# Layer 1's gate and up projections by Strassen's algorithm in a two-layer diffusion block: seven half products for eight

## The chip, the cores and the metric

The kernel runs on one core of one Trainium2 chip. The metric is the device time of one execution in microseconds (us). Profiles show the same kernel with the hardware profiler on, and give the span from the first to the last instruction.

## The reference, cut to what matters

Two layers work on 512 latent tokens and 256 context tokens of width 1024, in fp32. Each has a mixer (an mLSTM, a gating MLP, a convolution, then an output projection) and a SwiGLU feed-forward network (FFN). The second layer, layer 1, computes the mixer's output and the FFN for the latent tokens alone. What the change touches is this, with `FFN_HIDDEN` = 2816:

```python
def swiglu(h, w_gu, w_down):
    gate, up = jnp.split(h @ w_gu, 2, axis=-1)
    return (jax.nn.silu(gate) * up) @ w_down
...
x = x + g2 * swiglu(rmsnorm(x, norm2_g[l]) * (1.0 + sc2) + sh2, w_gu[l], w_down[l])
```

## The kernel before, in words

Everything lies transposed: features on the 128 partitions, tokens along the free dimension. A product of fp32 numbers is made of three passes of a faster format (`fp32r`): each operand is split into a rounded part `hi` and a remainder `lo`, and TensorE accumulates hi times hi, hi times lo and lo times hi in PSUM (L379, L380, L381, in `mm` inside `tiles`, L362). A weight tile of 128 columns by 1024 rows (8 slices of k, 128 rows each) arrives by DMA in a `raw` buffer (L314), ScalarE makes `hi` (L339) and VectorE makes `lo` (L320, `split_lo`). Three `raw` buffers and four `hi`/`lo` pairs (`spl`) rotate (`BUFFERS`, L217). The normalized activations lie in `HA` (latent) and `HB` (context), hi and lo each.

In layer 1 the 512 latent tokens form two groups of 256 (`GX0`, `GX1`), and every matmul there has 256 columns. The FFN has 22 hidden tiles of 128 (`NJ`); each takes one gate column tile and one up column tile (`gu_col`, L1569), so a pair of column tiles and both token groups cost 2 x 2 x 8 x 3 = 96 matmuls. `gu_evac` (L1579) then makes the hidden tile: silu on ScalarE (L1590), the product with up on VectorE (L1593), the split into hi (L1597, ScalarE) and lo (L1599, VectorE). The down projection is done in three runs over groups of hidden tiles (`FFN_GROUPS`, L35: 8, 7 and 7 tiles); `d_run` (L1603) makes 8 output tiles by 2 token groups a run, and VectorE adds each to the residual `xT` (L749). The last run starts with two output tiles side by side over k, so that the last hidden tile is read late.

The order of the work isn't written out by hand: `Plan` (L42) runs cooperating threads against a table of costs (`PE`, `DVE2`, `ACT` and so on) and writes each engine's instructions in the order in which its own clock serves them. TensorE follows the list of `steps`; VectorE and ScalarE take whatever thread is ready first. On the chip each engine then runs its list strictly in that order and waits on semaphores. The norm in front of the FFN is `norm` and `norm_lo` (L739, L714, L716); they write `HA`.

Of the kernel before, what the change touches and what calls it, by code (L numbers as in the profile page):

```python
# [14 lines left out]
P = 128  # L15
# [19 lines left out]
FFN_GROUPS = ((0, 8), (8, 7), (15, 7))  # L35
# [181 lines left out]
BUFFERS = {"ps": 8, "slot": 10, "raw": 3, "spl": 4, "pb": 4, "wi": 3, "cp": 1, "kk": 2, "hc": 2, "C0": 5, "C1": 5}  # L217
# [3 lines left out]
def backbone(ctx, tc, xT_d, cT_d, wmod_d, wb_d, wgv_d, wv_d, wout_d, wgu_d, wd_d, sw_d, sb_d, cv_d, rv_d, id_d, mk_d, out_d):  # L221
# [44 lines left out]
    # ---------------------------------------------------------------- weights  # L266
# [8 lines left out]
    def wsrc(key):  # L275
# [12 lines left out]
        if kind == "d":  # L288
            j0, n = FFN_GROUPS[key[2]]
            return wd_d[key[1], key[3], :, j0 * P:(j0 + n) * P], n, P  # L290
# [10 lines left out]
    def loader():  # L301
        for i, key in enumerate(ORDER):
            if key[0] == "x":
# [3 lines left out]
                continue  # L307
            src, a, b = wsrc(key)
# [14 lines left out]

    def splitter():
        for i, key in enumerate(ORDER):
            if key[0] == "x":
                continue
# [14 lines left out]
    prog = []  # L342

# [18 lines left out]
    def tiles(items, lead, lag, nk, src, wait=None, order=None, depth=3, wide=False, mid=None, after=None, ahead=2):  # L362
        """Steps of a run of 128-column products, tokens in one or two groups, `lead` ahead of `lag`.
        items: (weight key, evac, prio). With `wide`, the first tiles share one pass over k."""
# [42 lines left out]
        def multi(idx, pairs, state, spans):  # L407
            """pairs: (tile, group, first slot); one pass over the slots in spans, newly taken weights idx"""
# [187 lines left out]
    # ---------------------------------------------------------------- norms  # L596
# [161 lines left out]
    # ---------------------------------------------------------------- one layer  # L758
# [9 lines left out]
    def layer(l):  # L768
# [26 lines left out]
        # gates and the v half of the SGU, tokens on partitions  # L795
# [247 lines left out]
        # gated depthwise convolution  # L1043
# [92 lines left out]
        # mLSTM projections  # L1136
# [427 lines left out]
        steps.append(spawn_gs(l, 1))  # L1564
        steps += tiles([out_col(d) for d in range(KD)], gl, gg, KD, hsrc, lambda k, g: E("ys", g["t0"], k), YK, wide=True, ahead=AHEAD[1])

        hid, gups = {}, {}

# [9 lines left out]

        def gu_evac(j, g, pg, pu):  # L1579
# [23 lines left out]
        def d_run(gi):  # L1603
# [15 lines left out]
            def after(g):  # L1619
                st["dn", gi] = st.get(("dn", gi), 0) + 1  # L1620
                if st["dn", gi] == 2:
                    release("slot", nj)
# [172 lines left out]
```

## Time and profile before

| what | value |
|---|---|
| time, median of 3 runs | 1578.63 us (1578.39 to 1581.98) |
| span of the profiled execution | 1579.7 us (no separate time is listed for it) |
| instructions | 25862 |
| TensorE busy | 1549.2 us (98%), 10712 matmuls |
| VectorE busy | 845.3 us (54%) |
| ScalarE busy | 539.7 us (34%) |
| layer 1's FFN, about 1192 to 1570 us | 3168 matmuls of 256 columns |

Engines are PE (TensorE), PEld (its weight loads), DVE (VectorE), ACT (ScalarE), POOL and SP. Matmuls overlap in the pipe: one of 256 columns is shown with 0.28 us, while the next begins 0.11 to 0.12 us later, so the count of matmuls in a window says more than their busy time. The same holds to a lesser degree for VectorE and ScalarE, whose neighbouring instructions overlap by some 0.1 us. A wait is shown in brackets behind the instruction, with what ended it.

### The profile page before, as it was taken

What the parts mean: (1) busy time and instruction counts of PE and PEld (TensorE: products, weight loads), DVE (VectorE), ACT (ScalarE), POOL (GpSimd) and SP (SyncE); (2) the same over time, 40 slices, a digit from 0 to 9 for tenths busy, and PEclk for the clock granted to TensorE, in tenths of its full rate; (3) what the DMA queues carried; (4) which work ended last, traced back from release to release, by engine and by line L of the source; (5) the groups of instructions that cost most, each with busy time, mean ns of one, the idle gap of its engine ahead of it and who ended that gap; (6) DMA issues with size and microseconds to landing.
All of it is one profiled execution on the core that took longest, in us unless ns stands there. A gap on an engine that the chain in (4) does not pass through costs nothing.

```text
span 1579.7 us, 25862 instructions
## 1 busy us (share of the span) xinstructions
PE 1549.2 (98%) x10712; PEld 1386.1 (88%) x10712; DVE 845.3 (54%) x1739; ACT 539.7 (34%) x1055; POOL 32.0 (2%) x50
## 2 busy tenths in 40 slices
PE   5999999999999999999999999999999999999998
PEld 4887889889888888888888888788999999999997
DVE  5359877456655555344444363686766334334334
ACT  4332367534222212221122233426745321231333
POOL 0000010000000000000000000000100000000000
PEclk9999999999999999999999999999999999999999
DMA  9343345312333334333343122213332232223222
GB/s 327 118 131 118 121 131 159 120 59 68 107 120 128 113 107 144 134 108 101 132 151 121 52 83 81 87 55 113 103 107 81 94 94 94 94 88 99 96 83 66
DMA packets 68209, 173.22 MB, mean 110 GB/s; under 512 B 7052, under 2 KB 18428, under 8 KB 68092
## 3 DMA queue, kind: packets, MB, share of 16 engines
q1 hardware_dynamic: 65324, 170.15, 33.3%
q8 instruction: 84, 1.38, 0.4%
q10 hardware_dynamic: 2768, 1.42, 0.3%
q14 instruction: 33, 0.27, 0.1%
HBM read 169.34 MB, written 2.21 MB: 109 GB/s over the span
## 4 chain that ended last, share of the span: by engine, by line
PE 95%; DVE 2%; DMA 1%; issue 1%; ACT 0%; SPq 0%; POOLq 0%; POOL 0%; DVEq 0%
PE mm L379 27%; PE mm L380 27%; PE mm L381 27%; PE vp L1150 2%; PE vp L1152 1%; PE vp L1151 1%; PE stp L1287 1%; PE num L1371 1%; PE num L1374 1%; PE modps L501 1%; PE gvp L823 1%; PE gvp L824 1%; PE gvp L825 1%; DVE lo L320 1%; PE sT L1350 1%
## 5 line engine op out<-in xcount | busy, mean ns | idle before, releaser
L379 PE MATMUL mm<-HA,hi 128*128 128x256 f32 (+1 forms) x1568 | 525.3, 335 | 0.0
L380 PE MATMUL mm<-HA,hi 128*128 128x256 f32 (+1 forms) x1568 | 516.7, 330 | 2.4 <-DVE HA L716 1.8
L381 PE MATMUL mm<-HA,lo 128*128 128x256 f32 (+1 forms) x1568 | 516.2, 329 | 0.4 <-DVE lo L320 0.4
L320 DVE TENSOR_TENSOR lo<-raw,hi 128x1024 fp32r<-128x1024 f32 (+2 forms) x202 | 240.4, 1193 | 299.6 <-ACT hi L339 292.3
L339 ACT CAST hi<-raw 128x1024 fp32r<-128x1024 f32 (+2 forms) x202 | 206.3, 1024 | 565.7 <-PE mm L380 302.3
L381 PEld LDWEIGHTS mm<-HA,lo 128*128 128x128 f32 x1568 | 295.9, 189 | 30.6 <-DVE lo L320 0.6
L380 PEld LDWEIGHTS mm<-HA,hi 128*128 128x128 f32 x1568 | 296.2, 189 | 26.9 <-DVE HA L716 2.7
L379 PEld LDWEIGHTS mm<-HA,hi 128*128 128x128 f32 x1568 | 294.6, 188 | 28.7 <-issue 4.3
L379 PE MATMUL mm<-hid,hi 128*128 128x256 f32 (+1 forms) x704 | 218.7, 311 | 0.0
L381 PE MATMUL mm<-hid,lo 128*128 128x256 f32 (+1 forms) x704 | 217.5, 309 | 0.0
L380 PE MATMUL mm<-hid,hi 128*128 128x256 f32 (+1 forms) x704 | 217.2, 308 | 0.0
L379 PE MATMUL mm<-HB,hi 128*128 128x256 f32 x592 | 170.0, 287 | 0.0
L380 PE MATMUL mm<-HB,hi 128*128 128x256 f32 x592 | 164.6, 278 | 0.0
L381 PE MATMUL mm<-HB,lo 128*128 128x256 f32 x592 | 164.5, 278 | 0.0
L749 DVE SCALAR_TENSOR_TENSOR xT<-mm,modc,xT 128x256 f32<-128x256 f32 (+1 forms) x128 | 69.9, 550 | 160.1 <-PE mm L381 159.1
L379 PEld LDWEIGHTS mm<-hid,hi 128*128 128x128 f32 x704 | 132.7, 188 | 8.2 <-issue 0.8
L381 PEld LDWEIGHTS mm<-hid,lo 128*128 128x128 f32 x704 | 132.4, 188 | 7.7
L380 PEld LDWEIGHTS mm<-hid,hi 128*128 128x128 f32 x704 | 132.4, 188 | 7.5
L379 PEld LDWEIGHTS mm<-HB,hi 128*128 128x128 f32 x592 | 111.3, 188 | 8.1 <-issue 4.6
L380 PEld LDWEIGHTS mm<-HB,hi 128*128 128x128 f32 x592 | 111.9, 189 | 3.0 <-DVE HB L716 0.2
L381 PEld LDWEIGHTS mm<-HB,lo 128*128 128x128 f32 x592 | 111.2, 188 | 0.0
L573 DVE SCALAR_TENSOR_TENSOR macc<-raw,csil,macc 128x512 f32<-128x512 f32 x140 | 101.5, 746 | 0.6
(230 smaller groups left out, 1534.4 us busy)
## 6 DMA issues: line engine op xcount, KB each, us to landing
raw<-in_wmod SPq DMA_DIRECT2D x96, 512.0 KB, 3.8
raw<-in_wgu SPq DMA_DIRECT2D x88, 512.0 KB, 3.5
raw<-in_wb SPq DMA_DIRECT2D x36, 512.0 KB, 3.7
raw<-in_wd SPq DMA_DIRECT2D x32, 448.0 KB, 3.3
pbt<-dr SPq DMA_DIRECT2D x40, 256.0 KB, 3.4
raw<-in_wout SPq DMA_DIRECT2D x16, 512.0 KB, 3.6
raw<-in_wd SPq DMA_DIRECT2D x16, 512.0 KB, 3.6
raw<-in_wv SPq DMA_DIRECT2D x8, 512.0 KB, 3.9
```

Of the source, the lines that this page charges most:

```text
L320: dve.tensor_tensor(lo, r, hi.bitcast(F32), ALU.subtract)
L339: act.copy(hi, RAW[i])
L379: pe.matmul(o, lhsT=hi[:, k, :], rhs=hh, start=(j == 0), stop=False)
L380: pe.matmul(o, lhsT=hi[:, k, :], rhs=hl, start=False, stop=False)
L381: pe.matmul(o, lhsT=lo[:, k, :], rhs=hh, start=False, stop=(j == nk - 1))
L501: pe.matmul(p[32 * c:32 * c + 32, 0:256], lhsT=csil[:, k, :], rhs=s[:, c, :], start=(k == 0), stop=(k == KD - 1), skip_group_check=True)
L573: dve.scalar_tensor_tensor(a[:, g, :], s[:, i, :], c, a[:, g, :], ALU.mult, ALU.add)
L749: dve.scalar_tensor_tensor(x, p[:, 0:n], MODC[l][:, v, d, g:g + 1], x, ALU.mult, ALU.add)
L823: pe.matmul(out, lhsT=hh, rhs=hi[:, kk, :], start=(k == 0), stop=False)
L824: pe.matmul(out, lhsT=hh, rhs=lo[:, kk, :], start=False, stop=False)
L825: pe.matmul(out, lhsT=hl, rhs=hi[:, kk, :], start=False, stop=(k == KD - 1))
L1150: pe.matmul(out, lhsT=hh, rhs=hi[:, kk, :], start=(k == 0), stop=False)
```

## The change

Layer 1's first two hidden tiles (`NPLAIN`) are computed as before. For each of the other 20, the gate and the up tile form a matrix of two by two blocks (two column tiles by two halves of k), the activations another (two halves of k by two token groups), and the product is made in Strassen's way (Winograd's form of it): seven products of 4 slices of k by 3 passes, 12 matmuls each, so 84 for 96. The pieces are:

- `pair_sums` (new, L343): loads both raw tiles of a pair, makes four sums of weight quarters in place on VectorE (128x512 each), and splits three full tiles (U1, U2, U3) and one half tile (U4, kept in a part of `HA` that is free after the plain tiles).
- `t_forms` (new, L1725): once, makes the four sums of activation quarters (four 128x1024 additions of hi and lo, then four sums, then four splits on ScalarE and VectorE), after the norm has ended. They lie in `HB` and in memory that was slots before.
- `pair_steps`, `pair_end`, `product` (new): the order of the seven products in TensorE's list. Three PSUM banks a pair, A, B and C. Products 1, 6, 7 and 4 accumulate into A one after the other, and between them ScalarE copies A's state out (`copy_out`, L1840); product 5 and the closing product go to C, product 2 to B. VectorE joins the copies with B and C (`join_one`, L1858; L1855). The end of a pair stands behind the first product of the next.
- `pair_out` (new, L1866): a last sum, silu over 512, two products on VectorE, the split of the hidden tile over 512.
- The down projection runs over four groups of 6, 6, 5 and 5 hidden tiles; the first three are woven into four pairs each, so that twelve pairs carry pieces of it between their products and eight don't.
- Buffers: `raw` 3 to 4, `spl` 4 to 5, for the whole kernel, so the planner may load and split weights earlier in layer 0 too. An argument of the build, `dynamic_dma_scratch_size=1024`, makes the room.

TensorE's list goes from 10026 matmuls to 9786, VectorE's from 1741 instructions to 1936, ScalarE's from 1030 to 1103.

```diff
-FFN_GROUPS = ((0, 8), (8, 7), (15, 7))
+FFN_GROUPS = (((0, 8), (8, 7), (15, 7)), ((0, 6), (6, 6), (12, 5), (17, 5)))
+NPLAIN = 2
...
-BUFFERS = {"ps": 8, "slot": 10, "raw": 3, "spl": 4, "pb": 4, "wi": 3, "cp": 1, "kk": 2, "hc": 2, "C0": 5, "C1": 5}
+BUFFERS = {"ps": 8, "slot": 10, "raw": 4, "spl": 5, "hp": 0, "u4": 0, "pb": 4, "wi": 3, "cp": 1, "kk": 2, "hc": 2, "C0": 5, "C1": 5}
...
+    def pair_sums(key, us):
...
+        yield from cast(0, r1)
+        yield from cast(3, a22)
+        yield from low(0, r1)
+        yield from low(3, a22)
+        yield from add(a22, a21, a22)
+        yield from add(a21, a11, a21)
+        yield W(ev("u", key[:3], 1))
+        yield from cast(1, r2)
+        yield from add(a11, a22, a11)
+        yield from add(a12, a11, a12)
+        yield W(ev("u", key[:3], 2))
+        yield from cast(2, r1)
+        yield from low(1, r2)
+        release("raw")
+        yield from low(2, r1)
+        release("raw")
...
+        def t_forms():
+            for g in (gl, gg):
+                for k in range(KD):
+                    yield W(ev("h", l, 1, g["t0"], k))
+            yield W(E("ffnmem"))
+            f = st.pop("tf")
+            for x, q in enumerate(((0, 0), (0, 1), (1, 0), (1, 1))):
+                yield DVE2(1024)
+                dve.tensor_tensor(f[x], quarter(0, *q).bitcast(F32), quarter(1, *q).bitcast(F32), ALU.add)
...
+            def first(w):
+                yield A("ps")
+                q["A"], q["U1"] = ps("bA"), w
+                yield from product(q["A"], w, 0, (0, 0), True)
+                spawn(copy_out(j, 0), 0.6)
+
+            def fifth(w):
+                yield A("ps")
+                q["C"], q["U2"] = ps("bC"), w
+                yield from product(q["C"], w, 1, 0, True)
+
+            def sixth(w):
+                q["U3"] = w
+                yield W(E("cp", j, 0))
+                yield from product(q["A"], w, 0, 1, False)
+                spawn(copy_out(j, 1), 0.6)
...
+            def seventh():
+                yield W(E("cp", j, 1))
+                yield from product(q["A"], q["U2"], 0, 2, False)
+                release("spl")
+                spawn(copy_out(j, 2), 0.6)
+
+            out = [([key + (0,)], first)]
+            if before is not None:
+                out.append(pair_end(before))
+            return out + [([key + (1,)], fifth), ([key + (2,)], sixth), ([], second), ([], seventh)]
...
+                yield W(E("cp", j, 2))
+                yield from product(q["A"], w, None, 3, False)
+                U4.append(w)
+                release("u4")
+                yield W(E("join", j))
+                yield from product(q["C"], q["U3"], 1, (1, 1), False)
+                release("spl")
+                spawn(pair_out(j), 0.5)
...
+            blocks = [pair_steps(j, j - 1 if i else None) for i, j in enumerate(pairs)]
+            for gi, (j0, nj) in enumerate(fg[:-1]):
+                first, ds = j0 + nj - NPLAIN + 1, d_run(gi)
+                for b in range(4):
+                    part = ds[b * len(ds) // 4:(b + 1) * len(ds) // 4]
+                    blocks[first + b] = blocks[first + b][:2] + spread(blocks[first + b][2:], part)
```

What the planner makes of it is seen at three places of VectorE's list. The first is the start of layer 1's FFN, behind the last `lo` of the norm (L716 before, L790 now). Before, the evacuations of the first tiles (`s`, `hid`) and the splits of the next weights (`lo<-raw,hi`) follow:

```order
L716 SCALAR_TENSOR_TENSOR HA<-nt,modc_84,HA 128x256 x2
L1593 TENSOR_TENSOR s<-s,mm 128x256 x2
L1599 TENSOR_TENSOR hid<-s,hid 128x256 x2
L320 TENSOR_TENSOR lo<-raw,hi 128x1024 x2
L1593 TENSOR_TENSOR s<-s,mm 128x256
```

Now six wide additions (`tf`) and seven evacuations of the plain tiles (L1691, L1697) come first, and behind them these rows. `tf` are the activation sums, `HB<-tf,HB` the remainders of the first two of them, `raw<-raw` the weight sums of the first two pairs; the third row from the end is the remainder of U2 of the first pair, which TensorE's second Strassen product reads:

```order
L1749 SCALAR_TENSOR_TENSOR tf<-tf 128x1024
L1751 SCALAR_TENSOR_TENSOR tf<-tf 128x1024
L1691 TENSOR_TENSOR s<-s,mm 128x256
L354 TENSOR_TENSOR lo<-raw,hi 128x1024 x2
L354 TENSOR_TENSOR HA<-raw,HA 128x4x128 x2
L359 TENSOR_TENSOR raw<-raw 128x512 x4
L1741 TENSOR_TENSOR HB<-tf,HB 128x1024
L359 TENSOR_TENSOR raw<-raw 128x512 x4
L1741 TENSOR_TENSOR HB<-tf,HB 128x1024
L354 TENSOR_TENSOR lo<-raw,hi 128x1024
L1697 TENSOR_TENSOR ffn<-s,ffn 128x256
L354 TENSOR_TENSOR lo<-raw,hi 128x1024
```

So all activation sums and the weight work of two pairs stand in one line ahead of the second product's weights. The second place is one period of the pairs that carry no down projection. Before, VectorE had this between two tiles there:

```order
L1593 TENSOR_TENSOR s_11464<-s_11464,mm_11435 128x256
L1593 TENSOR_TENSOR s_11495<-s_11495,mm_11465 128x256
L1599 TENSOR_TENSOR hid_11303<-s_11464,hid_11303 128x256
L1599 TENSOR_TENSOR hid_11494<-s_11495,hid_11494 128x256
L320 TENSOR_TENSOR lo_11530<-raw_11404,hi_11529 128x1024
L320 TENSOR_TENSOR lo_11586<-raw_11425,hi_11585 128x1024
```

Now one period has the rows below, then one more addition and the split of the next U2. The first row waits for the closing product of one pair (bank `bC`), the second is U3 of the next pair, which the product after next on TensorE reads; `x_11697<-x_11697,bB` waits for the next pair's product 2, `d_11801` for its product 7:

```order
L1872 TENSOR_TENSOR x_11579<-x_11579,bC_11613 128x256
L354 TENSOR_TENSOR lo_11662<-raw_11492,hi_11661 128x1024
L354 TENSOR_TENSOR lo_11679<-raw_11569,hi_11678 128x1024
L1877 SCALAR_TENSOR_TENSOR x_11579<-bA_11563,x_11579 128x256
L354 TENSOR_TENSOR HA_70<-raw_11590,HA_70 128x4x128
L1880 SCALAR_TENSOR_TENSOR x_11579<-d_11680,x_11579 128x256
L359 TENSOR_TENSOR raw_11590<-raw_11590 128x512
L1862 TENSOR_TENSOR x_11697<-x_11697,bB_11765 128x256
L359 TENSOR_TENSOR raw_11590<-raw_11569,raw_11590 128x512
L1886 TENSOR_TENSOR ffn_10735<-x_11579,ffn_10734 128x512
L359 TENSOR_TENSOR raw_11569<-raw_11590,raw_11569 128x512
L1855 TENSOR_TENSOR d_11801<-d_11801,bC_11731 128x256
```

Splits, sums and joins are interleaved, and rows that wait for TensorE stand ahead of rows that TensorE will wait for. The third place is the passage to the last run of the down projection. Before, the last hidden tile needed one short evacuation (256 tokens):

```order
L320 TENSOR_TENSOR lo<-raw,hi 128x896 x2
L1593 TENSOR_TENSOR s<-s,mm 128x256
L1599 TENSOR_TENSOR hid<-s,hid 128x256
L749 SCALAR_TENSOR_TENSOR xT<-mm,modc_84,xT 128x256 x2
L627 TENSOR_TENSOR acc<-acc,sq 128x256
```

Now it needs `pair_out` over all 512 tokens, with the split of another weight tile in between:

```order
L1872 TENSOR_TENSOR x<-x,bC 128x256
L333 TENSOR_TENSOR lo<-raw,hi 128x640
L1877 SCALAR_TENSOR_TENSOR x<-bA,x 128x256
L1880 SCALAR_TENSOR_TENSOR x<-d,x 128x256
L1886 TENSOR_TENSOR ffn<-x,ffn 128x512
L823 SCALAR_TENSOR_TENSOR xT<-mm,modc_84,xT 128x256 x2
L701 TENSOR_TENSOR acc<-acc,sq 128x256
```

TensorE has 24 matmuls of the last run between the pair's closing product and the first that reads this hidden tile.

More of the change, by code (lines that the diff above doesn't have):

```diff
@@ new lines, in plain_done, with u4_free, product @@
+        def plain_done():
+            spawn(u4_free(), 0)
+            return
+            yield
+        def u4_free():
+            yield W(E("tread"))
+            for x in range(2):
+                U4.append(tuple(HA[:, w, 0:4, HM + x * P:HM + (x + 1) * P] for w in range(2)))
+            release("u4", 2)
+        def product(p, w, half, right, start):
+            hi, lo = w
+            if half is not None:
+                hi, lo = hi[:, 4 * half:4 * half + 4], lo[:, 4 * half:4 * half + 4]
+            if isinstance(right, int):
+                yield W(E("T", right))
+                rh, rl = TF[right]
+            else:
+                rh, rl = quarter(0, *right), quarter(1, *right)
+            o = p[:, 0:HM]
+            for k in range(4):
+                yield PE(HM, 3)
+                pe.matmul(o, lhsT=hi[:, k], rhs=rh[:, k], start=start and k == 0, stop=False, skip_group_check=True)
+                pe.matmul(o, lhsT=hi[:, k], rhs=rl[:, k], start=False, stop=False, skip_group_check=True)
+                pe.matmul(o, lhsT=lo[:, k], rhs=rh[:, k], start=False, stop=k == 3, skip_group_check=True)
@@ new lines, in join_one, with pair_out @@
+        def join_one(j):
+            q = pr[j]
+            yield W(E("cp", j, 0))
+            yield DVE2(HM)
+            dve.tensor_tensor(q["x"][:, 0], q["x"][:, 0], q["B"][:, 0:HM], ALU.add)
+            release("ps")
+            fire(E("one", j))
+        def pair_out(j):
+            q = pr.pop(j)
+            x, d = q["x"], q["d"]
+            yield from hid_slot(j)
+            yield W(E("one", j))
+            yield DVE2(HM)
+            dve.tensor_tensor(x[:, 1], x[:, 1], q["C"][:, 0:HM], ALU.add)
+            release("ps")
+            yield ACT(2 * HM, "silu")
+            act.activation(x, x, AF.Silu)
+            yield STT(HM)
+            dve.scalar_tensor_tensor(x[:, 0], q["A"][:, 0:HM], -1.0, x[:, 0], ALU.mult, ALU.mult)
+            release("ps")
+            yield STT(HM)
+            dve.scalar_tensor_tensor(x[:, 1], d, -1.0, x[:, 1], ALU.mult, ALU.mult)
+            release("pb")
+            xf = x.rearrange("p a b -> p (a b)")
+            yield ACT(2 * HM)
+            act.copy(hid[j][0], xf)
+            yield DVE2(2 * HM)
+            dve.tensor_tensor(hid[j][1], xf, hid[j][0].bitcast(F32), ALU.subtract)
+            release("pb")
+            for g in (gl, gg):
+                fire(E("hid", j, g["t0"]))
@@ L1642, in layer @@
             steps.append(spawn_gs(l + 1, 0))
+        else:
+            steps += gsteps
+            steps.append(([], plain_done))
+            pairs = list(range(NPLAIN, NJ))
+            blocks = [pair_steps(j, j - 1 if i else None) for i, j in enumerate(pairs)]
[4 more added lines that the diff above has]
+                    blocks[first + b] = blocks[first + b][:2] + spread(blocks[first + b][2:], part)
+            for b in blocks:
+                steps += b
+            steps.append(pair_end(pairs[-1]))
+            gi = len(fg) - 1
         steps.extend(d_run(gi))
```

189 lines of the change are left out of this document (165 added, 24 removed).

## The prediction

> **What bounds the kernel now.** First the page: its span, busy times and slices.
>
> ```profile
> span 1579.7 us, 25862 instructions
> ...
> PE 1549.2 (98%) x10712; PEld 1386.1 (88%) x10712; DVE 845.3 (54%) x1739; ACT 539.7 (34%) x1055; POOL 32.0 (2%) x50
> ...
> PE   5999999999999999999999999999999999999998
> ...
> DVE  5359877456655555344444363686766334334334
> ACT  4332367534222212221122233426745321231333
> ...
> PEclk9999999999999999999999999999999999999999
> ```
>
> TensorE is the bound from the first slice to the last. In the last ten slices, layer 1's FFN, VectorE and ScalarE are a third busy. The waits of TensorE say whether it is held up at all:
>
> ```profile
> PE modps L521 <- ACT sq L639: 16.5, 1, 16.5
> ...
> PE mm L380 <- DVE HA L716: 1.8, 3, 1.0
> ```
>
> The 16.5 us is the start; the 1.8 us lies where the FFN's norm ends. Inside the FFN there is no wait, so each matmul saved there is time saved at the pace of that stage. The windows give the pace (count behind PE, then PEld, DVE, ACT, POOL, clock):
>
> ```profile
> 1300.00:1400.00 100.00, 100.00 (x850) 100.00 (x849) 36.41 (x54) 25.75 (x38) 0.00 (x0) 1.00 0.29 95
> 1400.00:1500.00 100.00, 100.00 (x862) 100.00 (x862) 37.28 (x55) 25.76 (x39) 0.00 (x0) 1.00 0.30 96
> ...
> 1470.00:1520.00 50.00, 50.00 (x444) 50.00 (x443) 17.38 (x26) 15.45 (x27) 0.00 (x0) 1.00 0.31 98
> ```
>
> 100 us / 850 is 117.6 ns a matmul of 256 columns. One stretch of the same work runs at 50 us / 444 = 112.6 ns; what makes it quicker no view shows.
>
> **What is removed.** 20 pairs x (96 - 84) = 240 matmuls, which is just the difference of TensorE's two lists (10026 and 9786): 240 x 117.6 ns = 28.2 us. Against it, 76 more groups of matmuls begin (seven products a pair for four, one run more). 24 matmuls with one beginning at 850 in 100 us already contain it, so I count only 0.01 us for each further beginning: 0.8 us, an estimate, with bounds of nothing and three times that.
>
> **What is added on VectorE and ScalarE.** The prices, from the FFN's groups and, for 512 columns, from layer 0's:
>
> ```profile
> L320 DVE TENSOR_TENSOR lo<-raw,hi 128x1024 fp32r<-128x1024 f32 x45 | 55.1, 1226 | 114.1 <-ACT hi L339 114.1
> L339 ACT CAST hi<-raw 128x1024 fp32r<-128x1024 f32 x46 | 48.2, 1049 | 152.4 <-PE mm L380 152.4
> L749 DVE SCALAR_TENSOR_TENSOR xT<-mm,modc,xT 128x256 f32<-128x256 f32 x32 | 15.5, 484 | 42.0 <-PE mm L381 41.8
> L1593 DVE TENSOR_TENSOR s<-s,mm 128x256 f32<-128x256 f32 x37 | 15.4, 418 | 7.0 <-PE mm L381 5.8 <-ACT s L1590 1.2
> ...
> L1599 DVE TENSOR_TENSOR hid<-s,hid 128x512 fp32r<-128x512 f32 x22 | 15.2, 690 | 9.0 <-ACT hid L1597 8.9
> L1597 ACT CAST hid<-s 128x512 fp32r<-128x512 f32 x22 | 13.7, 621 | 76.9 <-DVE s L1593 76.8
> L1590 ACT ACTIVATE s<-mm 128x512 f32<-128x512 f32 x22 | 13.0, 592 | 0.0
> ```
>
> Neighbours overlap. The timeline shows it, and where the norm ends:
>
> ```profile
> 1162.96 2.36 DVE L320 TENSOR_TENSOR lo<-raw,hi 128x1024 fp32r<-128x1024 f32 x2 [0.48 <-ACT hi L339]
> ...
> 1208.27 0.48 DVE L716 SCALAR_TENSOR_TENSOR HA<-nt,modc,HA 128x256 fp32r<-128x256 f32 x1 [0.18 <-ACT HA L714]
> 1209.97 0.75 DVE L1593 TENSOR_TENSOR s<-s,mm 128x256 f32<-128x256 f32 x2 [1.21 <-ACT s L1590]
> ```
>
> Two of 1024 take 2.36 us, so the second adds 1.13; two of 256 take 0.75, the second adds 0.33. In a queue I therefore charge 1.14, 0.60 (0.690 less the same overlap) and 0.34 us for 1024, 512 and 256 columns, and 0.40 and 1.2 us for the three-operand form of 256 and 1024 (the last an estimate from 0.484 and 1.226).
>
> *A usual pair.* VectorE: three splits of 1024 (3.42), five pieces of 512 for U4 and the sums (3.00), three joins (1.02), two three-operand products (0.80), one split of 512 (0.60): 8.8 us. ScalarE, with 0.95 for 1024, 0.5 for 512 and 0.35 for 256 columns (estimates from 1.049, 0.621 and 0.592 in the same way): 3 x 0.95 + 3 x 0.5 + 3 x 0.35 = 5.4 us. TensorE: 84 x 117.6 ns = 9.9 us. In the twelve pairs with pieces of the down projection TensorE has up to 72 more matmuls (8.5 us) and VectorE 3.4 us (two splits of 768, four additions to the residual), so it is covered. The 16 additions to the residual of the fourth group, 16 x 0.40 us, lie in the same cover; so does the loading, 1 MB a pair in 9.9 us for 11.3. In the eight pairs without, VectorE has 1.1 us to spare, and what counts is order. After the closing product VectorE's list has the join with C (0.34), then U3's split (1.14), and TensorE reads that `lo` in the third matmul of the product after next: 14 x 117.6 ns = 1.65 us after, against 0.2 (the last matmul draining, which shows 0.28 us and is followed after 0.12) + 0.34 + 1.14 + 0.1 = 1.8. I take 0.2 us for five such pairs: 1.0 us; bounds nothing, and 12 us (1.5 us for each of eight, if nothing overlaps).
>
> *The start.* This is the largest cost. TensorE's place is known from the second `rstdb` of the norm:
>
> ```profile
> 1201.06 0.60 PE L692 MATMUL rstdb<-ident,rs 128*128 128x128 f32 x4
> ```
>
> Behind it stand 159 matmuls of the plain tiles, 12 of product 1 and 2 of product 5 before U2's `lo` is read: 1201.4 + 173 x 0.1176 = 1221.8 us. VectorE may begin the activation sums at 1208.7. Ahead of U2's `lo`, it included, stand eleven rows of 1024 (12.5), two three-operand rows of 1024 (2.4), seven evacuations (2.4) and ten rows of 512 (6.0), 23.3 us: 1232.0, and some 0.3 for the first evacuation's wait. So TensorE stands still for 10.5 us, with a few matmuls in between. Bounds: 7 (three rows less if waits of the planner fall well), 14 (full durations instead of overlapped ones). Of the rest of the activation sums nothing is late: T2 and T3 follow within 4 us, and are read 4 and 7 us after.
>
> A stall of that length touches the clock. The end of the trace shows what it does once TensorE rests, and the norm's short waits show no drop:
>
> ```profile
> 1190.00:1200.00 10.00, 8.15 (x65) 7.56 (x65) 8.43 (x20) 5.45 (x10) 0.70 (x1) 1.00 0.31 103
> ...
> 1572.00:1574.00 2.00, 0.78 (x5) 0.52 (x4) 0.24 (x2) 0.00 (x0) 0.69 (x1) 0.95 0.00 0
> 1574.00:1576.00 2.00, 0.00 (x0) 0.00 (x0) 2.00 (x7) 0.00 (x0) 0.00 (x0) 0.50 0.40 132
> ```
>
> The granted clock is 0.50 some 4 us after the last run of matmuls. If it takes as long to come back, 4 us at half speed lose 2 us. No row shows the return, so the bounds are nothing and 4 us. The Trainium skill ("TensorE: Matmul & The Clock Gate", Part 1: The HAM clock gate) says that an idle window of about 3.4 us halves the clock until a window of sustained work has passed; by it the loss is 1.7 us (half of 3.4) or, since windows run freely, up to twice that, an estimate from the page. The drop in the last rows agrees with it, and my 2 us would be 1.7 to 3.4.
>
> *The end.* The last pair's hidden tile is read 24 matmuls after the closing product, 2.8 us; its `lo` one matmul later, 2.9. Its chain: draining 0.2, the split weight tile that stands in between (ScalarE 0.7, VectorE until 1.75), two products (0.8), cast 0.62, split 0.69, handing over 0.1: 4.0 us. That is 1.1 us, bounds nothing and 2.5. Nothing was late there before.
>
> *Everything else.* More `raw` and `spl` buffers let the planner pull loads and splits forward in layer 0 (the first difference is a split of 816 columns ahead of the first context norm). TensorE waits there nowhere but in the first 36 us, so I take nothing, bounds 2 us either way. The pace is left at 117.6 ns; if all of the FFN ran at 112.6 it would save some 12 us more, if none did, the 2.5 us of the quick stretch (some 500 matmuls x 5 ns) would be lost.
>
> **The sum.** 28.2 - 0.8 - 1.0 - 10.5 - 2.0 - 1.1 = 12.8 us less. The span is 1579.7, 1.1 above the median of the runs; taken from the median, 1578.6 - 12.8 = 1565.8, so 1566 us.
>
> **The rivals.**
> 1. *The start is hidden and the saving comes whole.* The pair phase loses 3 us at most, or the quicker pace of 1470 to 1520 holds for longer: 1578.6 - 25 = 1554 us, 1548 to 1559. For it: VectorE is a third busy. Against: the 23.3 us in its list, all behind the norm. Chance 0.12.
> 2. *VectorE paces the pairs.* In the eight pairs without down projection full durations count: 3 x 1.23 + 6 x 0.69 + 3 x 0.42 + 2 x 0.48 = 10.0 us, already more than TensorE's 9.9, and six of the rows wait for TensorE or ScalarE in order. With half a us for each wait a pair takes 13.0, so 8 x 3.1 = 25 us are lost where I have 1.0, and the time is 1578.6 - 12.8 + 24 = 1590 us (1583 to 1596). It turns slower from 1.7 us lost in each of the eight. For it: each wait has something queued behind it on VectorE that TensorE needs soon. Against: the overlap in the timeline, and 1.1 us of slack. Chance 0.06; half of it, so that saving and loss cancel (1574 to 1583), 0.10.
> 3. *Small waits in the pairs bring the clock down.* At half clock the five first pairs alone cost 5 x 9.9 = 49 us: 1615. The Trainium skill names such an oscillation when TensorE idles between groups ("TensorE: Matmul & The Clock Gate", A second HAM failure mode). Against it: the window at 1190, with 1.8 us of waits in 10, kept 1.00. Chance 0.01.
>
> **How the numbers follow.** The forecast, 1559 to 1574, has 0.71; it is the likeliest, so 1566 us is the number. The range of 8 in 10 reaches from the upper part of rival 1 to the beginning of the case of no change: 1556 to 1575. A measurement of this kernel tells 0.3%, 4.7 us, from no change, so faster means below 1573.9: 0.71 + 0.12 = 0.83; same 0.10; slower 0.06 + 0.01 = 0.07.
>
> **What would show it.** In the profile after: some 10 us of TensorE waiting for a `lo` of line L354 between 1220 and 1235, with the clock below 1.00 in the window behind it; pairs without down projection 9.9 to 10.3 us apart, with VectorE about 90% busy; a wait of about 1 us for the last hidden tile (L1886). I am wrong if the first wait is under 5 us, if TensorE waits over 1 us in each pair, or if the stages ahead of 1190 differ by more than 2 us.

## The result, and the profile after

The changed kernel took 1569.51 us (median of 4 runs, 1568.44 to 1571.31), the kernel before 1580.31 us on the same chip (4 runs, 1578.39 to 1582.54): a ratio of 0.9925, with a 95% interval from 0.9909 to 0.9941. That is 10.8 us less. The profiled execution took 1569.28 us, with a span of 1567.5 where the kernel before had 1579.7.

The page of the changed kernel, its span, busy times and slices:

```profile
span 1567.5 us, 25687 instructions
...
PE 1525.9 (97%) x10472; PEld 1360.0 (87%) x10472; DVE 966.2 (62%) x1934; ACT 590.3 (38%) x1128; POOL 30.9 (2%) x50
...
PE   4999999999999999999999999999999799999997
...
PEclk9999999999999999999999999999999899999999
```

TensorE has 240 matmuls less, and between its first and its last slice only one, the 32nd, in which it is not full; the clock dips in the same slice. The waits of TensorE name what it stands for there:

```profile
PE bC L1785 <- DVE lo L354: 4.1, 1, 4.1
PE bC L1783 <- ACT hi L350: 3.8, 1, 3.8
...
PE bA L1785 <- DVE lo L354: 1.7, 1, 1.7
```

L350 and L354 make `hi` and `lo` of the pairs' weights. The windows around that place (TensorE's busy time and matmuls come first, the granted clock stands third from the end):

```profile
1210.00:1220.00 10.00, 10.00 (x91) 10.00 (x90) 9.74 (x15) 4.53 (x10) 0.00 (x0) 1.00 0.00 0
1220.00:1230.00 10.00, 4.39 (x34) 3.70 (x32) 9.97 (x14) 6.23 (x9) 0.00 (x0) 0.89 0.01 2
1230.00:1240.00 10.00, 5.90 (x34) 5.61 (x35) 8.36 (x10) 4.49 (x6) 0.00 (x0) 0.60 0.32 105
1240.00:1250.00 10.00, 10.00 (x90) 10.00 (x89) 7.11 (x11) 4.87 (x8) 0.00 (x0) 1.00 0.34 107
1250.00:1300.00 50.00, 49.94 (x423) 49.34 (x422) 41.08 (x66) 27.11 (x41) 0.00 (x0) 1.00 0.30 96
```

Two windows of 34 matmuls stand between windows of 90; from 1240 on TensorE is full again, with VectorE 82% busy beside it from 1250 to 1300. TensorE's timeline shows the three stops one by one; start, duration, instruction, and in brackets the idle time before it:

```profile
1222.11 0.28 PE L1784 MATMUL bA<-HA,hi 128*128 128x256 f32 x1
1224.11 0.39 PE L1785 MATMUL bA<-HA,lo 128*128 128x256 f32 x1 [1.73 <-DVE lo L354]
...
1225.25 0.28 PE L1785 MATMUL bA<-HA,lo 128*128 128x256 f32 x1
1229.34 0.58 PE L1783 MATMUL bC<-HB,hi 128*128 128x256 f32 x1 [3.81 <-ACT hi L350]
1229.99 0.58 PE L1784 MATMUL bC<-HB,hi 128*128 128x256 f32 x1
1234.67 0.58 PE L1785 MATMUL bC<-HB,lo 128*128 128x256 f32 x1 [4.10 <-DVE lo L354]
1235.05 0.42 PE L1783 MATMUL bC<-HB,hi 128*128 128x256 f32 x1
```

From the matmul at 1222.11 to the one at 1234.67 are 13 steps, 1.53 us of work at 117.6 ns: 11.0 us are lost. Behind that the matmuls take 0.42 us and stand 0.213 us apart until 1238.0 (half clock): the 16 steps from 1234.67 to 1238.14 take 3.47 us, 1.6 more than at 117.6 ns. VectorE's own timeline has no gap in the same stretch:

```profile
1211.14 1.22 DVE L1733 TENSOR_TENSOR tf<-HA 128x1024 f32<-128x1024 f32 x1
...
1222.84 2.35 DVE L354 TENSOR_TENSOR lo<-raw,hi 128x1024 fp32r<-128x1024 f32 x2
...
1233.40 1.22 DVE L354 TENSOR_TENSOR lo<-raw,hi 128x1024 fp32r<-128x1024 f32 x1
```

It begins the activation sums at 1211.14 and ends U2's `lo` at 1234.6, 23.5 us later. The end of the FFN, where the last hidden tile is read:

```profile
1529.54 0.28 PE L455 MATMUL mm<-ffn,lo 128*128 128x256 f32 x1
1529.91 0.38 PE L453 MATMUL mm<-ffn,hi 128*128 128x256 f32 x1
1530.64 0.38 PE L454 MATMUL mm<-ffn,hi 128*128 128x256 f32 x1 [0.34 <-DVE ffn L1886]
```

1.10 us for two steps of 0.118, and 0.22 for the next: 1.0 us lost. Between the two places TensorE loses more than 0.1 us at a time only at U3's `lo`. The third pair:

```profile
1256.90 0.28 PE L1784 MATMUL bA<-HB,hi 128*128 128x256 f32 x1
1257.23 0.39 PE L1785 MATMUL bA<-HB,lo 128*128 128x256 f32 x1
1257.46 0.28 PE L1783 MATMUL bA<-HB,hi 128*128 128x256 f32 x1
```

Two steps take 0.56 us for 0.235. No idle time stands in brackets, since a matmul is shown with 0.28 us although the next could begin after 0.12; only the starts tell. The same is seen at 1267, 1277 and 1369, the fourth, fifth and eleventh pair: 0.3 us each, 1.2 us together.

The landmarks put the sum together. From the second `rstdb` of the FFN's norm to the last one of the kernel, the kernel before needed 372.1 us (1201.06 to 1573.17) and the changed one 357.4 (1203.52 to 1560.88): 14.7 us less. Matmuls saved, 28.2; lost, 11.0 + 1.6 + 1.0 + 1.2 = 14.8; the difference is 13.4. The 1.3 us that are missing are pace: 372.1 us / 3168 is 117.5 ns a matmul before, (357.4 - 14.8) / 2928 is 117.0 now. But the second `rstdb` itself came 2.4 us later, and the first 3.6 us later (1195.16 for 1191.57), which my text had named as a sign of being wrong.

### The profile page after: what moved, and what is told of

Same layout as the page of the kernel before. It is cut to its first block, busy times and chain, and to the rows that moved or that the text cites. A ratio compares the mean times of both kernels' runs of the same rounds, so it can differ in the third digit from the quotient of the medians.

```text
span 1567.5 us, 25687 instructions
## 1 busy us (share of the span) xinstructions
PE 1525.9 (97%) x10472; PEld 1360.0 (87%) x10472; DVE 966.2 (62%) x1934; ACT 590.3 (38%) x1128; POOL 30.9 (2%) x50
## 4 chain that ended last, share of the span: by engine, by line
PE 94%; DVE 3%; DMA 1%; ACT 1%; issue 1%; SPq 0%; POOLq 0%; POOL 0%; DVEq 0%; ACTq 0%
PE mm L453 23%; PE mm L454 22%; PE mm L455 22%; PE bA L1785 2%; PE bA L1783 2%; PE bA L1784 2%; PE vp L1224 2%; PE vp L1226 1%; PE vp L1225 1%; PE bC L1785 1%; PE bC L1783 1%; PE bC L1784 1%; PE stp L1361 1%; PE num L1445 1%; PE num L1448 1%; PE modps L575 1%
## 5 line engine op out<-in xcount | busy, mean ns | idle before, releaser
L453 PE MATMUL mm<-HA,hi 128*128 128x512 f32 (+1 forms) x928 | 347.0, 374 | 1.7 <-ACT HA L1523 1.2
L454 PE MATMUL mm<-HA,hi 128*128 128x512 f32 (+1 forms) x928 | 337.9, 364 | 1.3 <-DVE HA L790 1.0
L455 PE MATMUL mm<-HA,lo 128*128 128x512 f32 (+1 forms) x928 | 337.4, 364 | 0.0
L412 ACT CAST hi<-raw 128x1024 fp32r<-128x1024 f32 (+5 forms) x170 | 165.9, 979 | 406.4 <-PE mm L454 148.3
L333 DVE TENSOR_TENSOR lo<-raw,hi 128x1024 fp32r<-128x1024 f32 (+5 forms) x170 | 192.5, 1135 | 159.9 <-ACT hi L412 151.9
L453 PEld LDWEIGHTS mm<-HA,hi 128*128 128x128 f32 x928 | 175.1, 189 | 31.4 <-issue 4.7
L455 PEld LDWEIGHTS mm<-HA,lo 128*128 128x128 f32 x928 | 174.5, 188 | 29.9
L454 PEld LDWEIGHTS mm<-HA,hi 128*128 128x128 f32 x928 | 175.0, 189 | 25.8 <-DVE HA L790 1.9
L453 PE MATMUL mm<-hid,hi 128*128 128x256 f32 (+1 forms) x352 | 119.6, 340 | 0.0
L455 PE MATMUL mm<-hid,lo 128*128 128x256 f32 (+1 forms) x352 | 118.7, 337 | 0.0
L454 PE MATMUL mm<-hid,hi 128*128 128x256 f32 (+1 forms) x352 | 118.4, 336 | 0.0
L454 PE MATMUL mm<-ffn,hi 128*128 128x256 f32 x352 | 99.1, 282 | 0.3 <-DVE ffn L1886 0.3
L453 PE MATMUL mm<-ffn,hi 128*128 128x256 f32 x352 | 99.1, 281 | 0.1
L455 PE MATMUL mm<-ffn,lo 128*128 128x256 f32 x352 | 98.4, 280 | 0.0
```

Of the source, the lines that this page charges most:

```text
L333: dve.tensor_tensor(lo, r, hi.bitcast(F32), ALU.subtract)
L412: act.copy(hi, RAW[i])
L453: pe.matmul(o, lhsT=hi[:, k, :], rhs=hh, start=(j == 0), stop=False)
L454: pe.matmul(o, lhsT=hi[:, k, :], rhs=hl, start=False, stop=False)
L455: pe.matmul(o, lhsT=lo[:, k, :], rhs=hh, start=False, stop=(j == nk - 1))
```

## The experiments

My theory was that VectorE's queue behind the norm makes the stop, and that the half clock follows from it. Its rivals: that VectorE has no room in the pairs either, and that the two more buffers disturb the stages ahead. Each kernel was timed beside the kernel before (1582.9 to 1583.7 us on these chips); ratios are to that.

**The buffers alone.** In the kernel before:

```
-BUFFERS = {... "raw": 3, "spl": 4, ...}
+BUFFERS = {... "raw": 4, "spl": 5, ...}
```

> The kernel before with the two more buffers alone (raw 3 to 4, spl 4 to 5, and the build's argument that makes room). Theory A, the buffers alone move the stages ahead of layer 1's FFN: the first rstdb of that FFN's norm comes 2.5 to 4 us later than in the kernel before (there 1191.6 us, in the changed kernel 1195.2), about half of it in the first 40 us, and the time is 2 to 4 us longer than the kernel before's. Rival: what the change spawns at its FFN is at fault, or the profiles only differ from each other by that much; then the landmarks agree within 1 us and the time within 1.5 us.

Measured: 1580.69 us, 0.9983 (0.9973 to 0.9992), so 2.6 us faster and not slower: theory A falls for the time. Its first `rstdb` came at 1193.14, 1.6 us later than before, as neither text said, and its FFN took 368.9 us for 372.1.

**The buffers late.** In the changed kernel:

```
+S = Plan({**BUFFERS, "raw": 3, "spl": 4})
...
 def spawn_ffn():
+    release("raw")
+    release("spl")
```

> The changed kernel, with the planner counting 3 raw and 4 spl buffers until layer 1's last projection and 4 and 5 from there; the memory and the build's argument stay as in the change. Theory A (the planner's reordering with more buffers costs the 3.6 us ahead of the FFN): the time is 2 to 4 us below the changed kernel's 1569.5, so 10.8 + 2 to 4 = 13 to 15 us below the kernel before, and the first rstdb of layer 1's FFN norm is within 1 us of the 1191.6 us before. Rival B (the build's argument or the memory's place costs it, not the order): the time stays at the changed kernel's within 1 us, and the first rstdb stays near 1195. The stall of 11 us for U2 stays in both.

Measured: 1568.08 us, 0.9904 (0.9890 to 0.9917). The ratio fits A, yet the first `rstdb` came at 1194.70, where A wanted 1192, and the FFN gives 0.7 us of the gain (356.7 us for 357.4). The interval overlaps that of the changed kernel, so the gain itself isn't certain. Nothing here shows the order ahead as the cause.

**The four groups alone.** In the kernel before, `FFN_GROUPS` of layer 1 as in the change:

> The kernel before with layer 1's down projection in four groups of 6, 6, 5 and 5 hidden tiles instead of three of 8, 7 and 7; everything else as before. My prediction counted nothing for the 16 additions to the residual and 0.2 us (16 groups of matmuls begun, 0.01 us each) for the fourth run: the time within 0.5 us of the kernel before. Rival: the shorter last run starts its last group with less work behind the last hidden tile, or the fourth run begins with stops of its own: 1 to 3 us longer.

Measured: 1579.77 us, 0.9973 (0.9961 to 0.9984), 3.5 us faster; I had expected nothing, and the rival 1 to 3 us more. Its FFN took 368.4 us for 372.1.

**The kernels once more.** What differs between the last three is the pace of the matmuls. To see what belongs to a program and what to an execution, both kernels were profiled a second time:

> The changed kernel once more, on the chip on which the other kernels of this round are timed. The kernel before and the one with the two more buffers alone came in between 1577 and 1585 us, and kernels with the same program ahead of layer 1's FFN reached that FFN's first rstdb between 1191.6 and 1195.2 us, so single profiles spread by some 3.6 us there. Theory A (the spread is between executions, not between programs): the ratio to the kernel before lies between 0.9895 and 0.9935, the time between 1567 and 1572 us, the first rstdb anywhere from 1192 to 1196. Rival (the change itself delays the stages ahead by 3.6 us): the first rstdb at 1195 or later again, 3 us or more behind the kernel before in each profile.

> The kernel before once more, for a second profile. In the profile of before a third (33%) of the FFN's matmuls with HA as operand stood 113 ns apart and the rest 118; with the two more buffers alone it was 74%, with the four groups alone 86%, in the changed kernel 67 and 77%, and the four groups alone were 0.27% faster than the kernel before. Theory A (which matmuls run at 113 ns is settled by the program's order): 25 to 45% again, the FFN from the second rstdb to the last 371 to 373 us, and no difference in the time. Theory B (it is settled anew in each execution): 50% or more in this profile, the FFN 368 to 370 us, and the time still as before's median, since the runs average over it.

Measured: the changed kernel 1570.89 us, 0.9923 (0.9908 to 0.9938), first `rstdb` 1193.69, as its theory A allowed, FFN 357.4 us again; the kernel before 1582.51 us, 0.9995 (0.9985 to 1.0005), first `rstdb` 1191.80, FFN 372.1 again. The FFN of the kernel before agrees with theory A of its text (371 to 373 us). Windows of the kernel before in its second profile:

```profile
1210.00:1300.00 90.00, 90.00 (x767) 90.00 (x766) 33.52 (x51) 29.08 (x51) 0.00 (x0) 1.00 0.30 94
1345.00:1425.00 80.00, 80.00 (x681) 80.00 (x680) 27.78 (x42) 23.37 (x40) 0.00 (x0) 1.00 0.30 91
1465.00:1525.00 60.00, 60.00 (x531) 60.00 (x531) 20.58 (x32) 18.57 (x32) 0.00 (x0) 1.00 0.30 93
```

and the third of them in its first one, where the other two have 767 and 681 matmuls again:

```profile
1465.00:1525.00 60.00, 60.00 (x532) 60.00 (x531) 20.81 (x32) 18.60 (x32) 0.00 (x0) 1.00 0.28 92
```

They agree to one matmul: 117.4 ns in the first two stretches and 113 in the third. The kernel with the buffers alone has the same list of matmuls in the FFN, and another pace in the second stretch:

```profile
1345.00:1425.00 80.00, 80.00 (x707) 80.00 (x706) 28.50 (x43) 23.32 (x40) 0.00 (x0) 1.00 0.31 94
```

So the pace belongs to the program, repeats itself, and changes with edits elsewhere. The changed kernel repeats itself less exactly: the same 58 us of its FFN, from 1242.00 and from 1240.55, have 493 and 496 matmuls, and over the whole FFN the two profiles differ by 0.05 us. Pace is also a good part of the 3.6 us ahead of the FFN. One window of the changed kernel, and behind it the same of the kernel with the earlier preparation (below), whose lists of matmuls are the same up to there:

```profile
1150.00:1190.00 40.00, 38.48 (x325) 38.08 (x324) 25.33 (x52) 19.28 (x40) 0.00 (x0) 1.00 0.33 106
```

```profile
1150.00:1190.00 40.00, 38.47 (x336) 38.07 (x335) 26.32 (x54) 19.17 (x40) 0.00 (x0) 1.00 0.32 105
```

Eleven matmuls less in 40 us are 1.3 us; the changed kernel had 325 in its second profile too. The rest is spread between executions of one kernel: the `rstdb` ahead of 380 us stood at 373.82 and 372.11 in the two profiles of the changed kernel, and at 371.66 before. The record shows where it comes from. The same window of the changed kernel in its first profile and in its second:

```profile
30.00:40.00 10.00, 8.41 (x94) 6.09 (x83) 6.61 (x15) 3.66 (x8) 0.00 (x0) 0.83 1.09 366
```

```profile
30.00:40.00 10.00, 8.60 (x109) 6.38 (x97) 7.71 (x18) 4.39 (x9) 0.00 (x0) 1.00 1.09 365
```

In the first TensorE had half clock for 3.4 us there (0.83 in ten), in the second none. The matmuls of the first are 0.4 us behind those of the second at 32 us, 1.9 behind at 37, and still 1.5 at the FFN's norm. The profiles of six other kernels, among them those with the buffers alone and with the groups alone, have the same 0.83; neither profile of the kernel before has it. So of the 3.6 us about 1.5 are this spell and 1.3 the pace.

**The preparation of the first pairs moved forward.** The core of it:

```
-spawn(pair_sums(key, us), 0)
+spawn(pair_sums(key, us), {NPLAIN: 0.52, NPLAIN + 1: 0.7}.get(key[2], 0))
...
+for x in range(2):
+    yield A("hp")
+    pc = st["hp"].pop(0)
+    u = tuple(y.rearrange("p (k c) -> p k c", k=4) for y in pc)
...
+    U4.append(u)
...
+yield from form(0, 0)
+yield from tsum(3, 1, 1)
...
+yield from form(1, 0)
...
+yield from form(2, 1)
+yield from tsum(2, 1, 0)
...
+if before is None:
+    return out + [([], second), ([key + (1,)], fifth), ([key + (2,)], sixth), ([], seventh)]
```

> The changed kernel, with the preparation of the first pairs moved forward: the first two U4 tiles lie in free hidden-tile memory, so that the first pair's weight sums needn't wait until TensorE has left the plain tiles; the activation sums are formed in the order in which they are read (T0, T1, T2, T3), and product 2 of the first pair stands ahead of its product 5. The computation is the same. Theory A (the 10.9 us stop for U2's lo is VectorE's queue behind the norm, and the half clock behind it follows from the stop): VectorE now has the first pair's U1 and U4 ready ahead and U2's lo some 12 us after the norm's end instead of 23; what is left is 3 us of waiting at T2 and 3 us at T3, because all the work (about 26 us of VectorE from the norm's end to T3's lo) still outlasts the matmuls (20 us); the granted clock stays at 1.00 in every window from 1200 to 1300. Sum: 12.4 us of stop and half clock become 5 to 7, so 5 to 8 us below the changed kernel's 1569.5. Rival (the order of VectorE's list doesn't matter, its total work between the norm and T3 does): the same 10 us of stop in other places, within 2 us of the changed kernel.

Measured: 1573.83 us, 0.9940 (0.9928 to 0.9953): by the ratios not faster but 2 to 3 us slower than the changed kernel, with an FFN of 363.0 us for 357.4 in the profile. Windows:

```profile
1220.00:1230.00 10.00, 7.45 (x61) 7.05 (x60) 10.00 (x14) 4.10 (x8) 0.00 (x0) 1.00 0.32 105
1230.00:1240.00 10.00, 7.14 (x36) 6.65 (x37) 8.75 (x13) 4.20 (x6) 0.00 (x0) 0.71 0.00 1
1240.00:1250.00 10.00, 6.11 (x33) 5.91 (x33) 6.40 (x11) 3.34 (x4) 0.00 (x0) 0.67 0.23 66
```

and the first stops in TensorE's timeline:

```profile
1226.62 0.28 PE L1800 MATMUL bA<-HB,lo 128*128 128x256 f32 x1
1227.91 0.38 PE L1798 MATMUL bA<-ffn,hi 128*128 128x256 f32 x1 [1.02 <-ACT x L1872]
1229.83 0.39 PE L1799 MATMUL bA<-ffn,hi 128*128 128x256 f32 x1 [1.54 <-DVE ffn L1753]
...
1230.90 0.42 PE L1798 MATMUL bA<-ffn,hi 128*128 128x256 f32 x1
```

The stop for U2 of the first pair is gone, as expected. But 3 us lost in two pieces were enough for half clock from 1230.9 until TensorE stopped again at 1234; further stops of 2.0 and 0.9 us were followed by it once more, until 1241.0; a stop of 3.9 us (U2 of the second pair) brought another 4.7 us of it. In all 51 matmuls at half clock cost 4.9 us where the changed kernel lost 1.6, since there most of the half clock, 10.2 us by the windows above, fell on a TensorE that stood still. The stops together, 9.3 us of idle time for 9.6, are hardly shorter, just as the rival said. My expectation that shorter stops leave the clock alone was wrong.

**Three plain tiles.** The same with `NPLAIN = 3`:

> As the kernel with the earlier preparation, and three plain hidden tiles instead of two, 19 pairs. The computation is the same. It adds 12 matmuls (1.4 us) to TensorE's list and gives VectorE 11.3 us more of matmuls to work behind. Theory A (the cost of the start is VectorE's queue, and the half clock only follows stops of TensorE): U2's lo is ready some 6 us before it is read, T3's lo some 4 us; no stop over 0.5 us between 1205 and 1300, no window there with the clock below 0.98. The changed kernel lost 10.9 + 1.55 us there, so 12.4 - 1.4 = 11 us below it: about 1558, ratio to the kernel before 0.985 to 0.9875. Rival (the pairs themselves stop TensorE once the long stop no longer hides it, since the first pairs stand without down projection): waits of 1 to 4 us at the second and third pair, the clock at 0.6 to 0.9 for 10 us or more, and a time no better than 1567.

Measured: 1565.01 us, 0.9885 (0.9869 to 0.9902), 5.9 us below the changed kernel on that chip. That is half of what theory A wanted. The stop at the first pair is gone; of TensorE's waits over 0.5 us one was left there:

```profile
PE bC L1800 <- DVE lo L355: 4.2, 1, 4.2
```

It stands at 1245.6, at U2 of the second pair, with 3.2 us of half clock behind it. In VectorE's list that `lo` stood behind rows of the third pair, to which I had given the earlier turn.

**The second pair first.** The weight sums' priority is 0.52, 0.51, 0.52, 0.52 for the first four pairs, 0 for the rest:

> As the kernel with three plain tiles and the earlier preparation, with one difference in the order of VectorE and ScalarE: the weight sums of the second pair come ahead of those of the third to fifth, so that U2's lo of the second pair stands ahead of the first pair's closing join in VectorE's list. The computation is the same. Theory A (the 4.2 us stop at 1246 is the second pair's U2 behind 6 us of the third pair's rows): no stop over 0.7 us between 1205 and 1300 and the clock 1.00 in every window there; 4.2 of stop and 1.1 of half clock go, so 5 us less than the 1565.0 us of the kernel without this difference, ratio to the kernel before 0.984 to 0.987. Rival (VectorE's work is too much for the first three pairs, whatever the order): the stop moves to the third pair, 3 us or more at its U2, and the time stays within 2 us of 1565.

Measured: 1561.07 us, 0.9862 (0.9847 to 0.9876). Windows:

```profile
1230.00:1240.00 10.00, 9.54 (x84) 9.34 (x82) 10.00 (x14) 4.45 (x8) 0.00 (x0) 1.00 0.34 107
1240.00:1250.00 10.00, 9.80 (x85) 9.61 (x84) 9.13 (x17) 5.94 (x10) 0.00 (x0) 1.00 0.33 105
1250.00:1300.00 50.00, 49.94 (x428) 49.74 (x427) 38.30 (x60) 24.30 (x38) 0.00 (x0) 1.00 0.36 112
```

No stop over 0.5 us, the clock at 1.00, VectorE full for 10 us and still in time. Theory A holds. This version beats both kernels: some 22 us below the kernel before and, by the ratios, 9 to 10 below the change. The step from the kernel ahead of it, some 4 us, is order alone; what the third plain tile and the earlier preparation each give can't be told apart.

**The same with late buffers.**

> The same with the planner counting 3 raw and 4 spl buffers until layer 1's last projection. The kernel with that count on the change as it stands had a ratio of 0.9904 to the kernel before, the change itself 0.9923 and 0.9925, with intervals that touch. Theory A (the order ahead of the FFN makes no difference that can be measured): within 2 us of the kernel without it. Rival (the buffers held back save 2 to 3 us in layer 0, hidden in single profiles by their spread): 2 to 3 us less, and the first rstdb of layer 1's FFN norm earlier by as much.

Measured: 1561.47 us, 0.9863 (0.9848 to 0.9878). No difference: theory A.

**More work for VectorE in each pair.** Behind the start of `pair_out`, with `range(2)` or, in a second kernel, `range(6)`:

```
+                spawn(extra(), 0.9)
...
+        def extra():
+            for _ in range(2):
+                yield DVE2(512)
+                dve.tensor_tensor(CX[:, :, 0:256], CX[:, :, 0:256], CX[:, :, 0:256], ALU.max)
```

> The changed kernel with two more VectorE instructions of 512 columns a pair (a maximum of a part of memory with itself, which changes nothing that is computed), about 1.2 us in VectorE's queue. In the changed kernel's profile VectorE waits some 1.6 us a pair for the closing product where no down projection runs. Theory A (my 8.8 of 9.9 us): the slack takes the 1.2 us, the time is 0 to 3 us longer than the changed kernel's on the same chip. Rival 1 (the order leaves no slack): 0.7 us or more in each of eight pairs, 6 us and up, and with stops like that also a lower clock between 1240 and 1290. Rival 2 (there is far more room than I counted): 0, and the same with six such instructions.

> The same with six such instructions a pair, about 3.6 us. Theory A by the count alone: 8.8 + 3.6 - 9.9 = 2.5 us too much in each of the eight pairs without down projection, 20 us longer, while the twelve others hide it. Theory B (stops of 1 to 4 us, repeated, halve the granted clock as they did in the kernel with the earlier preparation, where 2.5 us of waits at 1227 to 1230 were followed by 10 us at half clock): on top of the 20 us the matmuls between the stops run at 213 ns for a good part of the eight pairs; at half clock throughout a pair would take 84 x 0.213 = 17.9 us for 9.9 and no longer wait for VectorE, so up to 8 x 8 = 64 us; I expect 30 to 60 us longer, with the clock at 0.5 to 0.8 between 1240 and 1330. Rival 2 (much room): under 5 us.

Measured: 1577.01 us, 0.9959 (0.9945 to 0.9974), with two; 1593.19 us, 1.0063 (1.0047 to 1.0080), with six: 6.1 and 22.3 us above the changed kernel on that chip. With six, theory A's count of 20 us came out by luck. The pairs without down projection lost 6 us more than in the changed kernel, not 20: the third to fifth stop for 0.4 to 0.5 us each with the clock at 1.00, the eleventh for 2.0 us. The pairs with down projection, which A thought covered, lost 15.4 us more: four stops of 2.0 to 2.3 us for a `lo`, a few shorter ones, and half clock behind two of them. At 1411 the reason can be read: that `lo`, of U2, stands in VectorE's list behind the join that waits for the closing product of the pair before, and behind one of the added rows. Theory B's low clock between 1240 and 1330 came only in two spells of 3.4 us, from 1308.6 and from 1329.1. With two, the first five pairs have no new stop and the sixth one of 0.7 us; two more, of 2.0 us for a `lo` and 0.8 us for a join, stand further on, and 15 matmuls at half clock (1.4 us) follow the longer. So 6.1 us is as much as rival 1 said, yet not in each pair: most have room for 1.2 us more, and the order decides where it can't be used.

The kernel with six also shows what stop halves the clock. Two stops of the same 2.02 us; behind the first, half clock from 1308.7 to 1311.9:

```profile
1307.19 0.38 PE L1785 MATMUL bC<-HB,lo 128*128 128x256 f32 x1 [2.02 <-DVE lo L354]
...
1308.34 0.28 PE L1785 MATMUL bC<-HB,lo 128*128 128x256 f32 x1
1308.45 0.28 PE L453 MATMUL mm<-ffn,hi 128*128 128x256 f32 x1
```

and behind the second none:

```profile
1411.44 0.38 PE L1785 MATMUL bC<-HB,lo 128*128 128x256 f32 x1 [2.02 <-DVE lo L354]
```

What tells them apart is how the stop lies in steps of 3.41 us. Every spell of half clock that ends inside a profile here lasts one to four such steps, and within one profile their starts lie whole steps apart (here 1308.6, 1329.1, 1380.3). Cut by these steps, the two places are:

```profile
1305.20:1308.60 3.40, 1.41 (x12) 1.41 (x13) 3.40 (x5) 1.34 (x3) 0.00 (x0) 1.00 0.11 12
1308.60:1312.00 3.40, 3.40 (x19) 3.40 (x18) 2.42 (x5) 0.62 (x1) 0.00 (x0) 0.51 0.92 339
```

```profile
1407.60:1411.00 3.40, 1.83 (x16) 1.62 (x14) 3.10 (x6) 2.31 (x3) 0.00 (x0) 1.00 0.01 2
1411.00:1414.40 3.40, 2.96 (x25) 2.96 (x26) 3.40 (x6) 0.00 (x0) 0.00 (x0) 1.00 0.57 176
```

The first stop lies in one step and leaves 2.0 us of it idle; the second is shared by two steps, with 1.6 and 0.4. In layer 1's FFN, from 1200 to 1545 us in all profiles here, each full-clock step with 1.9 us or more of idle time was followed by half clock, and none with 1.7 or less. The limit isn't that sharp elsewhere: around 1150 steps with 1.5 us were followed by it in two profiles, and steps with 1.5 to 1.7 us in others not.

**The places of T0 to T3 exchanged.**

```
-TF[i] = (bufs[2 * i], bufs[2 * i + 1])
+TF[i] = (bufs[2 * i ^ 4], bufs[2 * i + 1 ^ 4])
```

> The changed kernel with the places of the activation sums exchanged: T0 and T1 in the memory that was slots, T2 and T3 in HB. The computation and the order are the same. In the changed kernel products 7 and 4 (T2 and T3, in slots) start their matmuls 118.2 ns apart in every pair, while those of HA and HB stand at 113.6 ns in most pairs and at 117 to 118 in the others. Theory A (the place of the moving operand sets the pace): products 5 and 6 now take 118 ns in every pair, products 7 and 4 are at 113.6 in some; the time within 2 us. Rival (the product sets it, or the bank, since both stand in the midst of what accumulates into A): products 7 and 4 stay at 118.2, products 5 and 6 as before.

Measured: 1569.79 us, 0.9916 (0.9900 to 0.9933), no difference in the time. The first matmul of product 6 (T1, now in slots) and of product 7 (T2, now in HB), each with the first behind its twelve:

```profile
1308.52 0.28 PE L1783 MATMUL bA<-ffn,hi 128*128 128x256 f32 x1
1309.93 0.28 PE L453 MATMUL mm<-ffn,hi 128*128 128x256 f32 x1
...
1315.54 0.28 PE L1783 MATMUL bA<-HB,hi 128*128 128x256 f32 x1
1316.90 0.28 PE L453 MATMUL mm<-ffn,hi 128*128 128x256 f32 x1
```

1.41 us / 12 = 117.5 ns and 1.36 / 12 = 113.3: in the same pair of the change it was 113.3 for product 6 and 117.9 for 7. So the place of the moving operand has a part in the pace. It isn't all: product 6 stayed quick in four pairs, product 4 stayed slow in all (120 ns, T3 now in HB), and the closing product went from 113.5 in most pairs to 117.8 in all without having been touched. Theory A holds for products 5 and 7 and most of 6; what else decides stays open.

## Why the prediction was right, step by step

- *240 matmuls at 117.6 ns, 28.2 us:* right. What stays of the FFN went at 117.0 ns for 117.5, which saved 1.3 us more; the prediction left the pace alone and named a quicker one only as a possibility.
- *76 more beginnings, 0.8 us:* nothing. In the rows above, 1308.34 to 1308.45, a group follows another in 0.11 us like any matmul.
- *U3's `lo` late in five pairs, 1.0 us:* 1.2, 0.3 in each of four pairs. VectorE is 82% busy from 1250 to 1300 (41.08 of 50 us in its window), not 90. The charge by neighbours' overlap was right; full durations (rival 2) were not.
- *The start, 10.5 us for U2's `lo`:* 11.0. The 23.6 us that I counted in VectorE's list were 23.5. I had one stop in mind; it came in three, for U1's `lo`, U2's `hi` and U2's `lo`, since all three hang on one queue. That the queue is the cause is shown by the kernel with the second pair first: its rows come in time for each read, stop and half clock are gone, and 9 to 10 us with them, although a third plain tile costs 1.4. Moving rows forward without that tile's cover had only moved the stops.
- *Half clock, 2.0 us:* 1.6. The return takes 3 us of work; I had taken 4, guessed from the fall. The Trainium skill ("TensorE: Matmul & The Clock Gate", Part 1: The HAM clock gate) says that an idle window of about 3.4 us lowers the clock, that as long a busy one restores it, and that the windows run freely. The spells here, whole multiples of 3.41 us, agree with the second and third. Stops of 2.0 us that lower the clock at one place and not at another agree with free-running windows, but not with 3.4 us of idleness as the least: here 2.0 us in one piece and 1.0 + 1.5 us in two were enough.
- *The last hidden tile, 1.1 us:* 1.0.
- *All else, nothing within 2 us:* the one step that failed in a profile. The FFN begins 2.4 us late in the first profile and 0.8 in the second (1202.06 for 1201.28). The reason that I had named, the loads pulled forward, isn't it: the kernel with the buffers alone isn't slower, and holding the buffers back changes nothing. It is 1.3 us of pace in one stretch and, in the first profile, some 1.5 us from a spell of half clock at 33 us, in the very stretch where the prediction knew of waits and still took nothing.
- *The rivals:* 1 (the start hidden) didn't come; it is what the kernel with the second pair first makes of the change. 2 didn't come: even with 3.6 us more work in each pair VectorE holds up only half of them. 3 didn't come in the change; in the kernel with the earlier preparation a few waits brought the clock to half three times within 20 us, and then it recovered.

So the mechanism was right in each step, and part of the closeness is luck. The terms that were too high (by 0.8, 0.4 and 0.1), those too low (by 0.5 and 0.2) and the 1.3 us of pace leave the FFN 1.9 us better than predicted (14.7 for 12.8). The late beginning takes 2.4 back in the first profile and 0.8 in the second: the spans are 12.2 and 13.9 us apart (1580.0 and 1566.1 in the second). The medians of the two comparisons, 10.8 and 12.8 us, are lower than that. In the second, the profiled execution was the shortest of six, and their times go by and large with their mean granted clocks: from 1567.87 us at 0.995 to 1574.54 at 0.990, where the kernel before had 0.996 to 0.998 throughout. So the changed kernel gets more half clock in some executions than in others, and the 1.6 us hold for the profiled one.

## What to carry to other kernels

Count, for a change of algorithm, the one-off work that its first step waits for, row by row in the queue of the engine that does it: here it ate 13 of 28 us while no later pair lost more than 0.3. When mending such a stop, remove it whole: cut into pieces of 1 to 4 us it cost more, because more matmuls then ran at half clock. And before a difference of 2 to 4 us between two kernels is laid to an edit, compare the matmul counts and the granted clock of equal windows: their pace can differ that much for another reason.

## What the hardware showed unexpectedly

Matmuls of the same form, with the clock at 1.00 and no wait, stood either 113 or 118 ns apart. Which it was belonged almost wholly to the program: two executions of the kernel before on different occasions agreed to one matmul in 532, those of the changed kernel to 3 in 496, while edits elsewhere (two more buffers, another grouping) moved it by 26 and 17 matmuls in the 80 us from 1345. The grouping alone made the kernel before 3.5 us faster, and its profile shows the quicker pace from 1300 to 1465, not in the rest of the FFN. The moving operand's place has a part in it; the rest is open, and wasn't tried further.

The clock, too, did not fall by the length of a stop alone: a stop of 2.02 us halved it where all of it lay in one step of 3.41 us, and left it alone where two steps shared it.
